# First products of a second model placed ahead of the last expert loads of the first, in a two-model kernel on one Trainium2 core

## The chip, the core and the metric

The kernel runs on one core of one Trainium2 chip. The engines that matter are TensorE (PE, with PEld for its weight loads), VectorE (DVE), ScalarE (ACT), GpSimd (POOL) and SyncE (SP, which here only issues DMA transfers, in program order, over 8 completion lanes named DMAHW0 to DMAHW7; transfers that GpSimd issues end on lanes named DMASW). A name that ends in _49 in a list of waits is a semaphore. The metric is the device time of the one core in microseconds (us), the median over several executions; lower is better.

## What is computed

Two models run one after the other, on 256 tokens of 1024 features, with 16 meta tokens ahead of them (272 columns). The first is a mixer of two attentions followed by a mixture of 32 experts (hidden size 512, two experts for each token); the second is a retention layer, a feed-forward layer, a latent attention and another feed-forward layer. Cut to what matters here:

```python
# first model
h = h + mixer(rmsnorm(h, g_mix), ...)
u = rmsnorm(h, g_ffn)                       # 256 tokens (+ 16 meta)
h = h + hier_moe(u, ...)                    # per expert: (silu(x @ w1) * (x @ w3)) @ w2
x = rmsnorm(h, g_final)[:, 16:]
# second model, first layer
h = concat(meta_2, x)
hn = rmsnorm(h, g_mix0)
proj = hn @ ret_w_in                        # q, k, v, gate of the retention
```

So between the two models stand two norms in a row, on the same sums: the mean square of the first model's output, and the mean square of that output after its gain.

## The kernel before

Activations are kept with features on the partitions, 8 blocks of 128 features by 272 columns (`h`). Weights of the mixer and of the second model are streamed as tiles of 128x128 floats, 16 tiles to a load of 1 MB (`raw`, class `Stream`) or 8 to a load of 512 KB (`rawh`); each is split into a high part on ACT (`wh`, L285) and a low part on DVE (`wl`, L286), and PE makes three products of 272 columns for each tile (L298 to L300). A tile of the activations is split likewise (`split_gain`, L289 on ACT and L290 on DVE, result `U`).

The experts (`moe`) run in 8 groups of 4 experts. A group takes 24 loads of 1 MB (`in_wm`, "chunks", 192 in all, numbered from 0): 16 for w1 and w3 (L983, 8 products each) and 8 for w2 (L1009, 8 products each). After each 4 chunks of w2 ACT copies the sum (`y`, L1012), PE scatters it to the tokens (L1016), and DVE adds it to two blocks of `h` at a time (L1018). Expert weights are not split. The chunks come through a ring of 16 slots made of three pools: `raw` (3), `raw2` (6) and `raw3` (7). `expert_fetch` (L1031) issues a chunk on SP's queue; a scheduler puts each issue where its slot becomes free.

After the second group stands a branch (L1027, L1028): when some expert has more than 32 tokens, `crowded` computes the rest. It doesn't run on these inputs, but its loads are on SP's queue, and every engine passes the branch.

In the last group (`g == 7`) `enter_meta` prepares the 16 meta columns, and `enter(b)` is called for each block as its last addition is done: it splits the block for the second model and makes two squares on ACT (L366 and L369, plain and scaled with the gain), which POOL adds up over the blocks (L373). The second model then opens with `retention`: it loads three chunks of the second stream (`in_ws2`) and two groups of constants, and `begin` (L312) computes the first four output blocks of the first projection from 8 feature blocks each: 32 tiles, 96 products, the 48 of feature blocks 0 to 3 first. Between them `enter_norms` sums the squares over the partitions (`colsum`, L383), takes the two inverse roots on DVE and spreads them over the partitions (L414). The fifth output block on PE can start when the rotations (`ro`, L1264, L1265) have freed the first accumulator.

The order on each engine is set when the kernel is built, by a scheduler that takes the program's order and the buffers' releases; the kernel's own code has no due times around the change.

## Time and profile before

| | |
|---|---|
| three runs, us | 1498.06, 1506.22, 1502.76 |
| median, us | 1502.76 |
| the profiled execution, us | 1498.93 |
| its span in the trace, us | 1497.1 |
| mixer | 0 to about 228 us |
| experts | about 229 to 692 us |
| second model | about 692 to 1497 us |
| PE busy over the span | 1314.9 us (88%) |
| bytes moved | 359.55 MB, mean 240 GB/s |

The profile is of one execution, 1498.93 us, that is 1.83 us longer than its span and 3.83 us below the median of the three. The page divides the span into 40 slices, of 37.4 us each. The mean figures over the whole span hide that the three stages have different limits, so each is to be read by itself. Places in the program are given by line, and times from the start of the span. A line "waits" gives who waited for whom, in total us, times and the longest; a bracket at the end of a row of the timeline gives the idle time of the engine before it and what ended that.

### The profile page before, as it was taken

What the parts mean: (1) busy time and instruction counts of PE and PEld (TensorE: products, weight loads), DVE (VectorE), ACT (ScalarE), POOL (GpSimd) and SP (SyncE); (2) the same over time, 40 slices, a digit from 0 to 9 for tenths busy, and PEclk for the clock granted to TensorE, in tenths of its full rate; (3) what the DMA queues carried; (4) which work ended last, traced back from release to release, by engine and by line L of the source; (5) the groups of instructions that cost most, each with busy time, mean ns of one, the idle gap of its engine ahead of it and who ended that gap; (6) DMA issues with size and microseconds to landing.
All of it is one profiled execution on the core that took longest, in us unless ns stands there. A gap on an engine that the chain in (4) does not pass through costs nothing.

```text
span 1497.1 us, 23804 instructions
## 1 busy us (share of the span) xinstructions
PE 1314.9 (88%) x9734; PEld 1051.7 (70%) x9734; DVE 724.4 (48%) x1417; ACT 528.3 (35%) x903; POOL 134.3 (9%) x165
## 2 busy tenths in 40 slices
PE   7999998776776666666999999999999999999997
PEld 7898993220221212104999999999999999899997
DVE  7866673110100101004666665766666865766654
ACT  5476651000000000004333443544444544544442
POOL 4010020000000000002121111100000211100001
PEclk9999998895787878778999999999999999999998
DMA  8443668999999999997434344454455433355551
GB/s 309 128 130 111 225 241 361 420 419 373 420 420 421 421 420 421 421 420 319 142 116 146 134 141 145 151 183 169 169 174 185 164 113 135 123 192 171 193 186 73
DMA packets 55266, 359.55 MB, mean 240 GB/s; under 512 B 6384, under 2 KB 7024, under 8 KB 15600
## 3 DMA queue, kind: packets, MB, share of 16 engines
q1 hardware_dynamic: 55152, 357.97, 63.2%
q8 instruction: 78, 1.28, 0.3%
q14 instruction: 36, 0.29, 0.1%
HBM read 356.90 MB, written 1.05 MB: 239 GB/s over the span
## 4 chain that ended last, share of the span: by engine, by line
PE 47%; DVE 2%; ACT 1%; issue 0%; POOL 0%; DVEq 0%; ACTq 0%; POOLq 0%
PE acc L298 14%; PE acc L300 14%; PE acc L299 14%; DVE wl L286 1%; ACT wh L285 1%; PE att L414 0%; PE att L1487 0%; PE att L1304 0%; PE att L1280 0%; PE att L383 0%; DVE U L290 0%; PE att L1306 0%; PE att L1397 0%; PE att L1294 0%; PE att L1305 0%
## 5 line engine op out<-in xcount | busy, mean ns | idle before, releaser
L298 PE MATMUL acc<-U,wh 128*128 128x272 f32 (+1 forms) x1456 | 424.0, 291 | 12.3 <-ACT U L289 7.2
L299 PE MATMUL acc<-U,wl 128*128 128x272 f32 (+1 forms) x1456 | 417.7, 287 | 2.5 <-DVE wl L286 2.5
L300 PE MATMUL acc<-U,wh 128*128 128x272 f32 (+1 forms) x1456 | 417.9, 287 | 0.0
L286 DVE TENSOR_TENSOR wl<-raw,wh 128x1024 fp32r<-128x1024 f32 x232 | 285.2, 1230 | 154.7 <-ACT wh L285 154.2
L285 ACT ACTIVATE wh<-raw 128x1024 fp32r<-128x1024 f32 x232 | 245.6, 1060 | 314.3 <-PE acc L300 211.2
L298 PEld LDWEIGHTS acc<-U,wh 128*128 128x128 f32 x1456 | 276.6, 190 | 17.6 <-ACT U L289 7.4
L299 PEld LDWEIGHTS acc<-U,wl 128*128 128x128 f32 x1456 | 275.9, 189 | 3.1 <-DVE wl L286 3.0
L300 PEld LDWEIGHTS acc<-U,wh 128*128 128x128 f32 x1456 | 275.9, 190 | 0.4
L983 PE MATMUL acc<-raw,U 128*32 128x512 f32 x1024 | 186.2, 820 | 91.0 <-DMA raw<-in_wm 87.3
L983 PEld LDWEIGHTS acc<-raw,U 128*32 128x32 f32 x1024 | 24.5, 124 | 238.1 <-DMA raw<-in_wm 214.7
L994 DVE TENSOR_TENSOR hid<-hid,acc 128x512 f32<-128x512 f32 x8 | 5.5, 688 | 258.1 <-PE acc L983 258.1
L300 PE MATMUL acc<-hl,wh 128*128 128x272 f32 (+1 forms) x352 | 99.5, 283 | 0.0
L299 PE MATMUL acc<-hh,wl 128*128 128x272 f32 (+1 forms) x352 | 99.3, 282 | 0.0
L298 PE MATMUL acc<-hh,wh 128*128 128x272 f32 (+1 forms) x352 | 99.1, 281 | 0.0
L1009 PE MATMUL att<-raw,ht 128*32 128x512 f32 x512 | 68.6, 635 | 28.7 <-DMA raw<-in_wm 25.1
L286 DVE TENSOR_TENSOR wl<-rawh,wh 128x512 fp32r<-128x512 f32 x112 | 80.5, 734 | 25.3 <-ACT wh L285 25.2
L285 ACT ACTIVATE wh<-rawh 128x512 fp32r<-128x512 f32 x112 | 68.2, 627 | 41.0 <-PE acc L300 24.9
L1018 DVE TENSOR_TENSOR h<-h,att 128x512 f32<-128x512 f32 x32 | 22.0, 688 | 123.9 <-PE att L1016 123.9
L298 PEld LDWEIGHTS acc<-hh,wh 128*128 128x128 f32 x352 | 66.4, 188 | 0.0
L300 PEld LDWEIGHTS acc<-hl,wh 128*128 128x128 f32 x352 | 66.1, 188 | 0.0
L299 PEld LDWEIGHTS acc<-hh,wl 128*128 128x128 f32 x352 | 66.1, 188 | 0.0
L373 POOL TENSOR_TENSOR s<-s,sq 128x256 f32<-128x256 f32 (+1 forms) x24 | 20.9, 886 | 493.3 <-ACT sq L369 492.8
(381 smaller groups left out, 1883.2 us busy)
## 6 DMA issues: line engine op xcount, KB each, us to landing
raw<-in_wm SPq DMA_DIRECT2D x192, 1024.0 KB, 19.9
raw<-in_ws SPq DMA_DIRECT2D x116, 1024.0 KB, 4.9
rawh<-in_ws SPq DMA_DIRECT2D x56, 512.0 KB, 3.9
const<-in_const SPq DMA_DIRECT2D x1, 1056.0 KB, 9.1
out<-Q SPq DMA_DIRECT2D x4, 256.0 KB, 2.5
h<-in_xt SPq DMA_DIRECT2D x2, 272.0 KB, 4.6
h<-in_xt SPq DMA_DIRECT2D x1, 544.0 KB, 6.6
small<-in_small SPq DMA_DIRECT2D x1, 512.0 KB, 6.2
```

The lines of the kernel that those rows point to most:

```text
L285: self.nc.scalar.activation(hi, src, AF.Copy)
L286: self.nc.vector.tensor_sub(lo, src, hi.bitcast(F32))
L298: mm(p[:, :n], wh, xh[:, kb, c0:c0 + n], start=kb == first, stop=False)
L299: mm(p[:, :n], wl, xh[:, kb, c0:c0 + n], start=False, stop=False)
L300: mm(p[:, :n], wh, xl[:, kb, c0:c0 + n], start=False, stop=kb == nkb - 1)
L373: self.nc.gpsimd.tensor_add(s[0], s[0], t)
L983: mm(p[32 * e:32 * e + 32], XG[:, j % 2, kb, c:c + 32], w[:, 512 * e:512 * e + 512], start=kb == 0, stop=kb == KB - 1)
L994: dve.tensor_mul(hid, hid, hh[1])
L1009: mm(p[32 * e:32 * e + 32], ht[:, f * P + e * 32:f * P + e * 32 + 32], w[:, 512 * e:512 * e + 512], start=f == 0, stop=f == 3)
L1018: dve.tensor_add(h[:, k:k + 2, NM:], h[:, k:k + 2, NM:], p.rearrange("p (j n) -> p j n", j=2))
```

## The change

- **Branch.** The loads of `crowded` are issued on GpSimd's queue instead of SP's.
- **Ring.** The pool of split weights (`wsp`, 3 pairs of tiles of 8) is made once for the whole kernel. Before, the mixer had its own with tiles of 4 and the second model its own. For this room the ring of chunks goes from 16 slots to 13 (`raw3` 7 to 4).
- **Second stream.** Its first 1 MB load is issued when 182 of the 192 expert chunks have been issued (`second_fetch`), in a slot of `raw`, and split (`Stream.split`) in the last group. Its next two loads are issued as halves of 512 KB after the last expert chunk.
- **Products.** `begin` becomes `begin_first` (the first four feature blocks of the first four output blocks, 16 tiles, 48 products), called before the last expert chunk in program order, and `begin_rest` (feature blocks 4 to 7, now block by block over the four outputs), called after the experts. The order of the tiles in memory changes with it (`_begin`).
- **Squares.** `enter` makes one square of a block instead of two, POOL adds nothing, and the sums over blocks and partitions are made by 16 small products of PE against a tile of two columns (ones and squared gain). The two spreads of the norms go into one accumulator, with two copies as before.
- **Small moves.** The meta columns' norm (`enter_meta`) is computed in group 6 instead of 7, the constants `const3` are loaded before the experts instead of after them, and in the mixer the splits are made 8 tiles at a time in two pieces.

```diff
-RAW, RAW2, RAW3 = 3, 6, 7
+RAW, RAW2, RAW3 = 3, 6, 4
...
 def _begin(blocks, cut):
-    return [b[:cut] for b in blocks[:4]] + [b[cut:] for b in blocks[:4]] + blocks[4:]
+    more = [b[k:k + 1] for k in range(cut, len(blocks[0])) for b in blocks[:4]]
+    return [b[:cut] for b in blocks[:4]] + more + blocks[4:]
...
+    def begin_first(self, ws, nkb, cut, xh, xl, cols, then=None, at=()):
         ps = [self.acc() for _ in range(3)] + [self.att()]
-        for i in range(8):
-            p, (c0, n) = ps[i % 4], cols[i % 4]
-            self.tiles(ws, p, range(cut) if i < 4 else range(cut, nkb), nkb, xh, xl, c0, n)
+        for i, (p, (c0, n)) in enumerate(zip(ps, cols)):
+            self.tiles(ws, p, range(cut), nkb, xh, xl, c0, n)
             if i in at:
                 next(then, None)
-        self.ready = [p[:, :n] for p, (_, n) in zip(ps, cols)]
+        self.begun = list(zip(ps, cols))
+
+    def begin_rest(self, ws, nkb, cut, xh, xl, then=None, at=()):
+        for kb in range(cut, nkb):
+            for p, (c0, n) in self.begun:
+                self.tiles(ws, p, [kb], nkb, xh, xl, c0, n)
+            if kb - nkb + 8 in at:
+                next(then, None)
+        self.ready = [p[:, :n] for p, (_, n) in self.begun]
...
+                if g == 6:
+                    self.consts_load("const3")
+                    self.enter_meta(m)
                 if g == 7:
-                    self.enter_meta(m)
+                    self.enter_start()
...
+                        if g == 7 and z == 1 and f == 3:
+                            self.begin_first(self.ws, KB, 4, self.u2[:, 0], self.u2[:, 1], [(0, T)] * 4)
                         w = self.expert_chunk()
...
                         if g == 7:
                             self.enter(k)
                             self.enter(k + 1)
+                            if k == 2:
+                                self.ws.split()
+                                self.ws.split()
...
+            self.ws.fetch(2, 2)
+            self.r1 = self.glob.tile([P, T], F32, name="s1")[:, :NX]
+            self.begin_rest(self.ws, KB, 4, self.u2[:, 0], self.u2[:, 1], self.enter_norms(self.r1), (4, 7))
 
     def expert_fetch(self):
 
+        if self.nraw == 192 - 192 % len(self.slots):
+
+            self.second_fetch()
...
+    def second_fetch(self):
+        self.ws = Stream(self, self.a["ws2"], 1856, self.raw, "raw", 16, 8)
+        self.ws.fetch(1)
...
-                    load = lambda c, i: nc.sync.dma_start(
+                    load = lambda c, i: nc.gpsimd.dma_start(
...
     def enter(self, b):
+
 
         x = self.h[:, b, NM:]
         self.split_gain(self.u2[:, 0, b, NM:], self.u2[:, 1, b, NM:], x, self.gg[:, b:b + 1])
-        self.square(self.s1, x, b)
-        self.square(self.s2, x, b, self.c("g_fin")[:, b:b + 1])
+        t = self.wk.tile([P, NX], F32, name="sq", bufs=4)
+        self.nc.scalar.activation(t, x, AF.Square)
+        if b == 0:
+            self.sums = self.att()
+        self.squares.append((b, t))
+        if b < 4:
+            self.sum_squares()
+
+    def sum_squares(self):
+        for b, t in self.squares:
+            for i in range(2):
+                self.nc.tensor.matmul(self.sums[:, 2 * i:2 * i + 2], t[:, i * P:(i + 1) * P], self.ones_g2[:, b],
+                                      start=b == 0 and i == 0, stop=True, skip_group_check=True)
+        self.squares = []
```

**SP at the branch.** Before, the join behind the branch waits for all eight DMA lanes, and the next expert chunk (L1036) stands behind it:

```order
L1028 UNCONDITIONAL_BRANCH [waits DMAHW0_49,DMAHW1_49,DMAHW2_49,DMAHW3_49,DMAHW4_49,DMAHW5_49,DMAHW6_49,DMAHW7_49]
L1027 ISA x2
L1036 DMA raw2_4380<-in_wm 128x2048 [waits DMAHW3_49,PE_49]
L1036 DMA raw3_4386<-in_wm 128x2048 [waits DMAHW4_49,PE_49]
L1036 DMA raw3_4392<-in_wm 128x2048 [waits DMAHW5_49,PE_49]
```

SP at the branch after the change (the branch is now L1064 and L1065, a chunk's issue L1079):

```order
L1065 UNCONDITIONAL_BRANCH
L1064 ISA x2
L1079 DMA raw2_4271<-in_wm 128x2048 [waits DMAHW4_49,PE_49]
L1079 DMA raw2_4277<-in_wm 128x2048 [waits DMAHW5_49,PE_49]
L1079 DMA raw2_4283<-in_wm 128x2048 [waits DMAHW6_49,PE_49]
L1079 DMA raw2_4289<-in_wm 128x2048 [waits DMAHW7_49,PE_49]
L1079 DMA raw2_4295<-in_wm 128x2048 [waits DMAHW0_49,PE_49]
L1079 DMA raw3_4301<-in_wm 128x2048 [waits DMAHW1_49,PE_49]
L1079 DMA raw3_4307<-in_wm 128x2048 [waits DMAHW2_49,DVE_49,PE_49]
L1079 DMA raw3_4313<-in_wm 128x2048 [waits DMASW7_49,DMASW6_49,DMAHW3_49,DMASW5_49,DMASW4_49]
```

The join has lost its waits; the seventh and eighth chunk behind it now wait for the other engines to have passed the branch.

**SP at the end of the experts.** Before, the last chunks of the experts (L1036), then the second stream's three loads (L238) and the constants (L273):

```order
L1036 DMA raw3_5574<-in_wm 128x2048 [waits DMAHW0_49,PE_49]
L1036 DMA raw3_5580<-in_wm 128x2048 [waits DMAHW1_49,PE_49]
L1036 DMA raw3_5586<-in_wm 128x2048 [waits DMAHW2_49,PE_49]
L238 DMA raw_5647<-in_ws2 128x2048 [waits DMAHW3_49,PE_49]
L238 DMA raw_5657<-in_ws2 128x2048 [waits DMAHW4_49,PE_49]
L238 DMA raw_5661<-in_ws2 128x2048 [waits DMAHW5_49,PE_49]
L273 DMA const3_5655<-in_const3 128x544 [waits DMAHW6_49,DMAHW2_49,PE_49]
L273 DMA const5_5659<-in_const5 128x2112 [waits DMAHW7_49,DMAHW1_49]
```

SP there after the change, from chunk 181 on (the second stream is L242, a chunk L1079); the "..." stands for six chunks' issues, which wait for a lane and PE:

```order
L1079 DMA raw3_5363<-in_wm 128x2048 [waits DMAHW1_49,PE_49]
L242 DMA raw_5369<-in_ws2 128x2048 [waits DMAHW2_49,PE_49]
L1079 DMA raw_5371<-in_wm 128x2048 [waits DMAHW3_49,PE_49]
L1079 DMA raw_5377<-in_wm 128x2048 [waits DMAHW4_49,PE_49]
L1079 DMA raw_5400<-in_wm 128x2048 [waits DMAHW5_49,DMAHW2_49,DVE_49]
L1079 DMA raw2_5406<-in_wm 128x2048 [waits DMAHW6_49,PE_49]
...
L1079 DMA raw3_5538<-in_wm 128x2048 [waits DMAHW4_49,PE_49]
L242 DMA raw_5570<-in_ws2 128x1024 [waits DMAHW5_49,PE_49]
```

One load of the second stream has moved ahead of ten expert chunks, and chunk 184 (`raw_5400`) takes its slot: it now waits for that load's own lane (DMAHW2) and for DVE, that is for the split of all 16 tiles.

**PE at the last chunk.** Before, the last products (L1009, chunk 191 in `raw3_5586`), the scatter of the last four blocks (L1016), and only then the second model's first products:

```order
L1009 MATMUL att_5567<-raw3_5586,ht_5500 32x512 [waits DMAHW2_49]
L1009 MATMUL att_5567<-raw3_5586,ht_5500 32x512 x3
L1016 MATMUL att_5594<-S_5502,y_5592 128x256 [waits Activation_49]
L1016 MATMUL att_5594<-S_5502,y_5592 128x256
L1016 MATMUL att_5614<-S_5502,y_5592 128x256 [waits PE_49]
L1016 MATMUL att_5614<-S_5502,y_5592 128x256
L298 MATMUL acc_5666<-U_5454,wh_5670 128x272 [waits Activation_49]
L298 MATMUL acc_5667<-U_5454,wh_5670 128x272
```

PE there after the change (second model's products L313 to L315, last chunk L1043 in `raw3_5538`, scatter L1050):

```order
L315 MATMUL att_5489<-U_5383,wh_5463 128x272
L313 MATMUL att_5489<-U_5383,wh_5463 128x272
L314 MATMUL att_5489<-U_5383,wl_5464 128x272
L315 MATMUL att_5489<-U_5383,wh_5463 128x272
L1043 MATMUL att_5467<-raw3_5538,ht_5395 32x512 [waits DMAHW4_49]
L1043 MATMUL att_5467<-raw3_5538,ht_5395 32x512 x3
L1050 MATMUL att_5546<-S_5397,y_5544 128x256 [waits Activation_49]
L1050 MATMUL att_5546<-S_5397,y_5544 128x256
L1050 MATMUL att_5558<-S_5397,y_5544 128x256 [waits PE_49]
L1050 MATMUL att_5558<-S_5397,y_5544 128x256
L313 MATMUL acc_5486<-U_5383,wh_5577 128x272 [waits Activation_49]
L314 MATMUL acc_5486<-U_5383,wl_5578 128x272 [waits DVE_49]
```

All 48 products of `begin_first` now stand ahead of chunk 191, the remaining ones behind the last scatter.

## Rows read from the trace of the kernel before

**Rows 1.** The page: mean DMA rate in each of the 40 slices; one row of the issues (KB each, median us to landing).
```profile
GB/s 309 128 130 111 225 241 361 420 419 373 420 420 421 421 420 421 421 420 319 142 116 146 134 141 145 151 183 169 169 174 185 164 113 135 123 192 171 193 186 73
...
raw<-in_ws SPq DMA_DIRECT2D x116, 1024.0 KB, 4.9
```
**Rows 2.** Windows by stage: length; busy PE, PEld, DVE, ACT, POOL; clock; DMA share; GB/s.
```profile
16.00:226.00 210.00, 208.98 (x1697) 194.36 (x1697) 150.69 (x360) 121.31 (x250) 29.86 (x34) 1.00 0.54 180
228.00:692.00 464.00, 316.80 (x1857) 88.50 (x1860) 51.73 (x151) 31.81 (x64) 1.92 (x3) 0.80 1.00 415
722.00:1497.00 775.00, 756.88 (x5986) 738.75 (x5986) 493.93 (x846) 348.80 (x541) 87.05 (x102) 0.99 0.45 153
```
**Rows 3.** Waits of SP's queue from 262 to 690 us: total us, times, longest.
```profile
SPq L1036 <- DMA raw<-in_wm: 324.3, 154, 3.5
SPq L1028 <- SPq L1028: 19.3, 3, 14.4
```
**Rows 4.** Windows around the branch, as in Rows 2.
```profile
340.00:350.00 10.00, 6.59 (x32) 0.67 (x24) 0.00 (x0) 0.00 (x0) 0.00 (x0) 0.50 0.64 238
350.00:390.00 40.00, 26.89 (x136) 5.17 (x132) 2.07 (x3) 1.88 (x3) 0.00 (x0) 0.67 1.01 420
```
**Rows 5.** Timeline of PE around the branch: chunk 52 and chunk 63.
```profile
339.61 1.94 PE L983 MATMUL acc<-raw,U 128*32 128x512 f32 x8 [1.32 <-DMA raw<-in_wm]
...
371.51 1.94 PE L983 MATMUL acc<-raw,U 128*32 128x512 f32 x8 [0.71 <-DMA raw<-in_wm]
```
**Rows 6.** Start of the experts: PE's first chunk (timeline); SP's waits, 226 to 262 us.
```profile
236.11 1.94 PE L983 MATMUL acc<-raw,U 128*32 128x512 f32 x8
...
SPq L1036 <- PE acc L983: 17.3, 10, 6.5
```
**Rows 7.** Timeline of the last groups: meta columns' norm, held-up products, last chunk.
```profile
675.60 0.15 DVE L403 TENSOR_SCALAR rs_v<-att 16x1 f32<-16x1 f32 x1 [0.37 <-PE att L383]
...
677.72 0.16 DVE L360 SCALAR_TENSOR_TENSOR rs_z<-rs_t,rs_y 128x1 f32<-128x1 f32 x1
...
680.33 5.07 PE L1009 MATMUL att<-raw,ht 128*32 128x512 f32 x32 [0.69 <-ACT ht L999]
...
691.77 1.07 PE L1009 MATMUL att<-raw,ht 128*32 128x512 f32 x8 [0.94 <-DMA raw<-in_wm]
```
**Rows 8.** Windows of 1 us, as in Rows 2: the clock behind 680 and 713 us.
```profile
683.00:684.00 1.00, 1.00 (x16) 0.26 (x12) 0.00 (x0) 0.00 (x0) 0.00 (x0) 0.87 1.02 426
...
713.00:714.00 1.00, 1.00 (x6) 1.00 (x6) 0.00 (x0) 0.16 (x1) 0.00 (x0) 0.51 1.00 426
```
**Rows 9.** Timeline from the last chunk to the fifth output block.
```profile
694.12 1.99 PE L1016 MATMUL att<-S,y 128*128 128x256 f32 x8 [1.28 <-ACT y L1012]
694.22 1.06 ACT L285 ACTIVATE wh<-raw 128x1024 fp32r<-128x1024 f32 x1 [0.15 <-DMA raw<-in_ws]
695.29 0.69 DVE L1018 TENSOR_TENSOR h<-h,att 128x512 f32<-128x512 f32 x1 [1.94 <-PE att L1016]
...
696.01 0.51 ACT L289 ACTIVATE U<-h,gg 128x256 fp32r<-128x256 f32 x1 [0.73 <-DVE h L1018]
...
696.76 1.22 DVE L286 TENSOR_TENSOR wl<-raw,wh 128x1024 fp32r<-128x1024 f32 x1
...
699.14 0.29 PE L298 MATMUL acc<-U,wh 128*128 128x272 f32 x1
...
700.14 0.29 PE L298 MATMUL acc<-U,wh 128*128 128x272 f32 x1
...
704.13 0.59 PE L298 MATMUL acc<-U,wh 128*128 128x272 f32 x1 [3.08 <-ACT wh L285]
...
704.75 0.85 PE L383 MATMUL att<-ones,s 128*128 128x1 f32 x4
...
719.53 1.05 PE L414 MATMUL att<-const,rs_z 128*128 128x128 f32 x8
...
722.59 0.36 PE L298 MATMUL acc<-U,wh 128*128 128x272 f32 x1 [2.01 <-DVE ro L1265]
```

More of the change, by code (lines that the diff above doesn't have):

```diff
@@ L237, in fetch, with split @@
             m, o = min(self.per, self.n - i) * P, i % 16 * P
-            self.k.nc.sync.dma_start(w[:, :m], self.src[i // 16][:, o:o + m])
+            e = m // pieces
+            for c in range(0, m, e):
+                self.k.nc.sync.dma_start(w[:, c:c + e], self.src[i // 16][:, o + c:o + c + e])
             self.q.append(w)
             self.c += 1
-    def next(self):
-        k, i = self.k, self.i
-        if i % self.per == 0:
+    def split(self):
+        k, j = self.k, self.j
+        if j % self.per == 0:
             if not self.q:
@@ L247, in next @@
             self.w = self.q.pop(0)
-        if i % self.cut == 0:
-            m = min(self.cut, self.n - i) * P
-            self.h = k.wsp.tile([P, self.cut * P], F32R, name="wh")
-            self.l = k.wsp.tile([P, self.cut * P], F32R, name="wl")
-            c = i % self.per * P
-            k.split(self.h[:, :m], self.l[:, :m], self.w[:, c:c + m])
+        h = k.wsp.tile([P, 8 * P], F32R, name="wh")
+        l = k.wsp.tile([P, 8 * P], F32R, name="wl")
+        n = min(8, self.n - j)
+        for o in range(0, n, self.cut):
+            m = min(self.cut, n - o) * P
+            c = (j % self.per + o) * P
+            k.split(h[:, o * P:o * P + m], l[:, o * P:o * P + m], self.w[:, c:c + m])
+        self.j += 8
+        self.parts.append((h, l))
+    def next(self):
+        i = self.i
+        if i % 8 == 0:
+            if not self.parts:
+                self.split()
+            self.h, self.l = self.parts.pop(0)
         self.i += 1
-        c = i % self.cut * P
+        c = i % 8 * P
         return self.h[:, c:c + P], self.l[:, c:c + P]
@@ L732, in mixer @@
             self.gens.append(stick())
+            qb = m.tile([P, 4, NX], F32, name="qi")
             for b in range(4):
@@ L1127, in enter_meta, with enter_start @@
         self.spread(self.row[:, :NM], self.norm_end(self.colsum([[s]], NM), NM, D, 1e-6), NM)
+    def enter_start(self):
+        self.u2 = self.glob.tile([P, 2, KB, T], F32R, name="U")
+        self.nc.vector.tensor_copy(self.h[:, :, :NM], self.meta)
+        self.split(self.u2[:, 0, :, :NM], self.u2[:, 1, :, :NM], self.meta_t)
     def enter(self, b):
```

66 lines of the change are left out of this document (34 added, 32 removed).

## The prediction, made before the changed kernel had run

> **What bounds the kernel now.** I read the windows by stage first, because the mean over the span mixes three limits. In the mixer PE is busy 208.98 of 210.00 us, in the second model 756.88 of 775.00; between them, for 464 us, it is busy 316.80 us while the DMA engines stand at a share of 1.00 and 415 GB/s [rows 2]. So the first and last stage are PE's and the experts are DMA's. The rates by slice say the same and show the hole: 420 GB/s in the experts' slices, but 373 in the tenth [rows 1]. Then I read who ends the waits of SP: in the experts it is the landing of older chunks (324.3 us), so that the next issue is never late, except at the branch, where it waits 19.3 us for its own lanes [rows 3]. Last came the timelines of the two seams, the branch and the end of the experts, since only at seams can this change take time out: a chunk of 1 MB at 421 GB/s takes 2.49 us, and nothing in the change makes one smaller. I use T for the moment at which chunk 191 lands, 691.77 in the trace [rows 7], and count to the start of the fifth output block, 722.59 [rows 9]: 30.8 us. Behind it PE is saturated as before, on the same work.
>
> **The change part by part: what moves T.**
>
> Branch: the join makes SP wait until every lane has landed, so the DMA engines run dry. From chunk 52 to chunk 63 PE's starts are 371.51 - 339.61 = 31.90 us apart [rows 5]; 11 chunks at 2.49 are 27.4, so the hole costs 4.5 us. The rate in 340 to 350 us, 238 GB/s, against 420 behind it [rows 4] says 10 x (1 - 238/420) = 4.3. The new join waits for nothing, and the first chunk that must wait for the other engines is the seventh behind it, with six transfers queued, that is 15 us of data. I take the whole 4.5 as gained (4.3 to 4.5).
>
> Second stream: its first 1 MB now goes ahead of ten chunks, in a stretch that DMA bounds: +2.49 us on T. [...]
>
> New wait: chunk 184 takes the slot of that load and waits for its landing and for both halves of its split, two of 1.06 us on ACT and 1.22 on DVE behind the second [rows 9], some 3.7 us with the handing over. Seven chunks stand behind it on SP, and PE waits for all of them. While SP waits, chunks 182 and 183 still land, the second of them 5.0 us behind the stream's load, so that the engines still have 1.3 us of work when the issue comes. A load that is issued alone lands after 4.9 us [rows 1]; 3.7 + 4.9 - 5.0 - 2.49 = 1.1 us late. The branch is the nearest row for a queue that restarts, and it lost more than its first landing; by its loss the term is 2.5. I take 2.0, nearer the branch; below it can go to 0 if the queue restarts under the rest of chunk 183, above to 4.5, the branch's whole price.
>
> Ring of 13 slots: before, SP waited at the start of the experts for PE's products 17.3 us in 10 waits [rows 6] without a gap in the transfers. With 13 slots the wait begins three chunks earlier, for the first chunk's products, which start at 236.11 us. Twelve chunks have been issued then and the last is still on its way. I take 0.2 us, range 0 to 1. Later PE consumes a chunk in 1.07 to 1.94 us [rows 5, 7] against 2.49 for a landing, and five chunks of slack beyond the eight in flight are 12.4 us, against 8.4 us from the landing of a group's last w3 chunk (T - 8 x 2.49 = 671.9) to its first w2 products at 680.33 [rows 7] in the last group, which alone has the meta norm in between.
>
> Sum for T: -4.5 + 2.5 + 2.0 + 0.2 = +0.2 us, between -2.0 and +3.5.
>
> **What moves between T and the fifth block.** Before, the path was: last products 1.07, sum copied and scatter at 694.12, addition, U of the last blocks from 696.01 on, mixed on ACT with sixteen squares and the first split; PE then starved for 3.08 us until 704.13, and ran the 96 products and 16 sums at the lower clock until 713 [rows 8, 9]. After, 48 products and half of the sums stand ahead of chunk 191, and the squares are halved. Steps, at full clock: chunk 187 lands four chunks ahead of T, at T - 10.0; 2.35 us from products to scatter, 1.2 to the addition, 0.7 addition, 0.5 for U [rows 7, 9]: first products at T - 5.3, at best T - 5.7 since the high part suffices. From there to the end of chunk 191 PE has 48 products of 0.125 (eight in 1.00 us [rows 9]), 6.0; four chunks of 1.07, 4.3; eight sums of 0.21, 1.7; the second half of a scatter, 1.0. Together 13.0: T + 7.3. So the first products don't fit before T, and the last chunk's products wait behind them. Then 1.28 to the scatter, 1.17 to the addition, 0.69 and 0.5 for addition and U [rows 9], less some 0.1 of overlap: T + 10.8. The other 48 products 6.0, eight sums 1.7, 0.6 of waiting for U of later blocks: T + 19.1. The norms' chain is 14 small operations of VectorE at 0.2 us (12 in 2.3 us [rows 7]), released by the last sums and mostly beside the last products; 0.8 remains. Spread 1.05, then 2.0 to the rotations' release [rows 9]: T + 23.0. Against 30.8 this gives 7.8 us.
>
> The weights of the later products come by two loads in halves behind the last chunk; the first half is wanted at T + 10.8 and has been landed for several us, so cost nothing. Removed additions on POOL and eight squares on ACT count only in that they no longer sit between U and the splits; they are in the steps above. The mixer's splits by eight, the earlier constants (544 floats on each partition, under a mixer that moves 180 GB/s [rows 2]) and the meta norm in group 6 lie beside PE or DMA work: 0, at most 1 us either way in the mixer, where PE is the bound and its products are the same.
>
> **The clock** decides between these steps and slower ones. The w2 products that began at 680.33 ran at the lower clock until 683.25 (0.87 in that slice: from 0.50 to 1.00), after 3 us without a pause; behind 704.13 the lower clock lasted until 714, over 9 us [rows 7 to 9]. Before the first products, PE will do one chunk of 1.07 to 1.94 us in each 2.49. I take 4 us of the lower clock from the first products on, near the 3 us case, since the products come without a pause: what takes 0.125 took about 0.227 there, so 1.8 us are lost. T + 24.8, a gain of 6.0 us.
>
> Total: +0.2 - 6.0 = **-5.8 us**. The profiled execution would go from 1498.93 to 1493.1; it is 3.8 us under the median of the runs, which would go from 1502.76 to **1497.0**.
>
> **Rivals.**
>
> Full clock and a short restart: the first products find the higher clock and chunk 184 costs the 1.1 us; T by -0.9, the tail by -7.8: -8.7 us, 1494.1. For it speaks that from 684 on the clock was full through the last chunk; against it that the held-up w2 products that brought it there are spread out now, as the meta norm leaves group 7.
>
> Half clock for longer: as behind 704.13, 9.4 us at the lower clock cost 4.2 instead of 1.8: -3.4 us, 1499.4. [...]
>
> The products in the way, on the other side: if the lower clock holds through all of it, the 48 products ahead of chunk 191 take 10.9, the four chunks 7.8, sums and scatter 3.6; the last chunk ends at T + 16.6, the last U at T + 20.9, the other products and sums 13.2 later, the fifth block at T + 39, 8 us later than now: +8.4 us, 1511.2. It turns to a loss once the lower clock lasts over some 17 us; against it, PE is then busy without a pause, and both rows end the lower clock within 10 us of that.
>
> The hole at the branch stays: SP stops there for another reason (the branch itself, or chunks 62 and 63 that wait for the others), and 4.5 isn't gained: -1.3, 1501.5. Against it: of the 19.3 us SP's wait is for its own lanes.
>
> **How the numbers follow.** Forecast 0.45; full clock 0.27; longer half clock 0.12; hole stays 0.08; products in the way 0.05; 0.03 for a loss from the ring or the restart above my bounds. The median of three runs here can be off by some 4 us, as the three lie over 8. Half a per cent, 7.5 us, is about what a measurement of this kernel can tell from no change: faster needs 1495.2. The forecast falls below that 3 times in 10, the full-clock case 2 in 3: 0.35 with a little of the rest. Slower 0.07, the rest 0.58. Range: 1489.0 (full clock, 5 us of scatter) to 1504.0 (hole stays, or longer half clock, with scatter).
>
> **What would show it.** In the changed kernel: no dip of the rate near 345 us and chunks at 2.49 us there; a hole of about 2 us in the transfers behind chunk 183; T within 3 us of 691.8; PE's products of the second model ahead of T, their spacing (0.125 or 0.227) telling the clock; the last chunk's products about 7 us behind its landing, and the fifth block 23 to 27 us behind it. Wrong would be: a rate under 400 GB/s elsewhere in the experts, last chunk's products over 15 us late, or a second model longer than 775 us.

## The result, and the profile after

The changed kernel took 1493.09 us (median of 5 runs, 1488.68 to 1497.56) against 1502.76 of the kernel before, run beside it (5 runs, 1498.06 to 1506.22): a ratio of 0.9941, 95% interval 0.9918 to 0.9964, a gain of 9.7 us. A second comparison on another chip (under a_after below) gave 0.9965 [0.9947, 0.9984], 5.9 us. The forecast was 5.8 us. The sum and the measurement thus lie close together, but the steps show that part of this is two errors of opposite sign.

The profiled execution took 1488.68 us, the fastest of the five. The page of the kernel after: its span and the DMA rate in each of 40 slices, to be put beside [rows 1]:

```profile
span 1487.0 us, 23794 instructions
...
GB/s 309 133 127 112 217 261 300 425 426 425 426 426 426 426 427 426 427 396 359 117 138 143 127 133 155 153 172 171 173 176 184 165 114 124 132 188 183 197 193 63
```

Three things differ from [rows 1]. The dip in the tenth slice is gone (373 before, 425 now). The seventh slice is lower (300 against 361) and the eighteenth has a new dip (396). And every full slice in between stands at 425 to 427, where before it stood at 419 to 421. Nothing in the change was meant to do the last.

Windows of the kernel after (columns as in [rows 2]): the experts and the second model as wholes, then the start of the experts, the branch, a long undisturbed stretch, and the end of the experts:

```profile
228.00:692.00 464.00, 327.12 (x1893) 95.05 (x1892) 54.57 (x160) 34.20 (x65) 0.00 (x0) 0.79 1.00 417
722.00:1487.00 765.00, 747.04 (x5938) 729.74 (x5937) 485.60 (x831) 347.78 (x540) 82.91 (x98) 0.99 0.45 154
...
230.00:240.00 10.00, 5.16 (x27) 2.83 (x31) 6.77 (x43) 0.80 (x3) 0.00 (x0) 0.66 0.81 315
240.00:250.00 10.00, 10.00 (x78) 3.94 (x71) 1.00 (x3) 1.15 (x3) 0.00 (x0) 1.00 0.96 360
...
340.00:350.00 10.00, 5.58 (x28) 0.64 (x24) 0.00 (x0) 0.00 (x0) 0.00 (x0) 0.66 1.01 424
380.00:640.00 260.00, 182.85 (x1024) 50.82 (x1020) 24.87 (x61) 14.18 (x26) 0.00 (x0) 0.79 1.01 426
660.00:670.00 10.00, 5.72 (x24) 0.60 (x24) 2.36 (x2) 2.00 (x2) 0.00 (x0) 0.50 0.81 318
...
665.00:666.00 1.00, 0.29 (x4) 0.20 (x8) 1.00 (x2) 0.20 (x1) 0.00 (x0) 0.50 0.66 279
```

340 to 350 us runs at 424 GB/s, where [rows 4] had 238. The two prices stand beside it: 315 and 360 GB/s in the first 20 us of the experts, and 318 behind chunk 183. The second begins ahead of the next issue: from 665 to 666 us, with only chunks 182 and 183 left to land, the rate is down to 279, and chunk 184 is issued at 666.68.

SP's waits in the kernel after (total us, times, longest), the first row from 226 to 262 us, the others from 262 to 700; they answer to [rows 3, 6]:

```profile
SPq L1079 <- PE acc L1012: 19.7, 12, 8.6
...
SPq L1079 <- DMA raw<-in_wm: 315.9, 153, 2.6
SPq L1079 <- DMA raw<-in_ws: 14.2, 1, 14.2
SPq L1079 <- PEq L1065: 6.8, 1, 6.8
SPq L1079 <- DVE wl L301: 3.5, 1, 3.5
```

At the branch SP still waits once, 6.8 us for PE's sequencer, but with six transfers queued that shows in no rate. At chunk 184 it waits for the second stream's load (14.2) and then 3.5 us for DVE's half of the split; the second is what empties the engines.

The timeline of the kernel after, at the start and the end of the experts (chunk 0; the splits, chunk 184's issue, chunk 187; first products; then, behind the last landing, the half-load's split, the last chunk and the fifth block):

```profile
237.11 1.91 PE L1012 MATMUL acc<-raw,U 128*32 128x512 f32 x8
...
663.20 2.00 ACT L300 ACTIVATE wh<-raw 128x1024 fp32r<-128x1024 f32 x2 [14.38 <-DMA raw<-in_ws]
664.29 2.36 DVE L301 TENSOR_TENSOR wl<-raw,wh 128x1024 fp32r<-128x1024 f32 x2 [31.89 <-ACT wh L300]
666.68 4.03 SPq L1079 DMA_DIRECT2D raw<-in_wm  x8
678.90 1.07 PE L1043 MATMUL att<-raw,ht 128*32 128x512 f32 x8 [1.42 <-DMA raw<-in_wm]
683.19 0.39 PE L313 MATMUL acc<-U,wh 128*128 128x272 f32 x1 [1.32 <-ACT U L304]
691.56 1.06 ACT L300 ACTIVATE wh<-raw 128x1024 fp32r<-128x1024 f32 x1 [4.13 <-DMA raw<-in_ws]
696.58 1.07 PE L1043 MATMUL att<-raw,ht 128*32 128x512 f32 x8
713.84 0.60 PE L313 MATMUL acc<-U,wh 128*128 128x272 f32 x1 [2.25 <-DVE ro L1328]
```

PE is busy with the early products when chunk 191 lands, so its landing has no row of its own. At 691.56 ACT starts on the half-load that stands right behind chunk 191; half a megabyte at 426 GB/s is 1.23 us, so T = 690.3. Against the 691.77 of [rows 7] T has moved by -1.5 us. The fifth block starts at 713.84, T + 23.5, against 722.59 and T + 30.8 [rows 9]. The whole gain up to the fifth block is 8.75 us: 1.5 on T, 7.3 behind it. The rest of the span, 773.2 us against 774.5, does the same work as before.

### The profile page after: what moved, and what is told of

Same layout as the page of the kernel before. It is cut to its first block, busy times and chain, and to the rows that moved or that the text cites. A ratio compares the mean times of both kernels' runs of the same rounds, so it can differ in the third digit from the quotient of the medians.

```text
span 1487.0 us, 23794 instructions
## 1 busy us (share of the span) xinstructions
PE 1317.5 (89%) x9750; PEld 1048.3 (71%) x9750; DVE 722.1 (49%) x1419; ACT 522.0 (35%) x895; POOL 124.4 (8%) x153
## 4 chain that ended last, share of the span: by engine, by line
PE 49%; DMA 22%; DVE 3%; ACT 1%; issue 1%; POOL 0%; SPq 0%; DVEq 0%; ACTq 0%; POOLq 0%
DMA raw<-in_wm 22%; PE acc L313 14%; PE acc L315 14%; PE acc L314 14%; DVE wl L301 1%; ACT wh L300 1%; PE att L440 1%; PE att L1550 0%; PE att L1367 0%; PE att L1343 0%; DVE U L305 0%; PE att L409 0%; PE att L1043 0%; PE att L1369 0%; PE att L1460 0%
## 5 line engine op out<-in xcount | busy, mean ns | idle before, releaser
L313 PE MATMUL acc<-U,wh 128*128 128x272 f32 (+1 forms) x1456 | 423.2, 291 | 11.6 <-ACT U L304 9.2
L315 PE MATMUL acc<-U,wh 128*128 128x272 f32 (+1 forms) x1456 | 416.6, 287 | 0.4 <-DVE U L305 0.4
L313 PEld LDWEIGHTS acc<-U,wh 128*128 128x128 f32 x1456 | 275.7, 189 | 17.6 <-ACT U L304 10.2
L315 PEld LDWEIGHTS acc<-U,wh 128*128 128x128 f32 x1456 | 275.4, 189 | 2.8 <-DVE h L1052 0.8
L315 PE MATMUL acc<-hl,wh 128*128 128x272 f32 (+1 forms) x352 | 99.4, 283 | 0.0
L313 PE MATMUL acc<-hh,wh 128*128 128x272 f32 (+1 forms) x352 | 99.1, 281 | 0.0
L1043 PE MATMUL att<-raw,ht 128*32 128x512 f32 x512 | 74.5, 680 | 23.6 <-DMA raw<-in_wm 19.4
L300 ACT ACTIVATE wh<-rawh 128x512 fp32r<-128x512 f32 x112 | 65.0, 624 | 33.8 <-PE acc L315 20.4
L313 PEld LDWEIGHTS acc<-hh,wh 128*128 128x128 f32 x352 | 66.3, 188 | 0.0
L315 PEld LDWEIGHTS acc<-hl,wh 128*128 128x128 f32 x352 | 66.2, 188 | 0.0
L313 PE MATMUL acc<-yh,wh 128*128 128x272 f32 (+1 forms) x192 | 56.7, 295 | 3.2 <-DVE h L362 3.2
```

The costliest lines, as they stand in the source:

```text
L300: self.nc.scalar.activation(hi, src, AF.Copy)
L313: mm(p[:, :n], wh, xh[:, kb, c0:c0 + n], start=kb == first, stop=False)
L315: mm(p[:, :n], wh, xl[:, kb, c0:c0 + n], start=False, stop=kb == nkb - 1)
L1043: mm(p[32 * e:32 * e + 32], ht[:, f * P + e * 32:f * P + e * 32 + 32], w[:, 512 * e:512 * e + 512], start=f == 0, stop=f == 3)
```

## The experiments

The theories. **By the steps:** the gain is the branch (about -4.4) and the end of the experts (-6 to -7), paid for with the moved load, its wait and a little of the ring. **Rivals:** the rate of 426 GB/s, which is worth 6.2 us over 445 us, comes from the ring, from the branch's queue or from elsewhere, and is the larger part of the gain; and the early products, which cost a load ahead of ten chunks, carry no gain at all.

**The kernel before again (e0_before),** unchanged, as the bound on what a comparison can show.

> The kernel before, unchanged, to have its transfer rate beside the others on one chip. After the change the experts' transfers ran at 426 GB/s against 420 in the trace of before, which over 445 us is some 6 us. If that is the chip or the day, this run shows 426 too, with the hole at the branch still there; if it comes from the change, it shows 420 again. Time: ratio 1.000 within 0.003.

Measured: 1501.82 us (10 runs), ratio 1.0003 [0.9990, 1.0016]. Its windows, for the comparisons on this chip:

```profile
230.00:240.00 10.00, 4.83 (x24) 2.70 (x24) 6.82 (x42) 0.80 (x3) 0.00 (x0) 0.66 0.93 365
240.00:250.00 10.00, 10.00 (x77) 3.88 (x76) 1.27 (x3) 1.15 (x3) 0.00 (x0) 1.00 1.02 428
...
380.00:640.00 260.00, 185.19 (x1013) 53.58 (x1008) 22.78 (x48) 14.17 (x26) 0.00 (x0) 0.77 1.01 421
```

**The short ring alone (e1_ring):** the kernel before with 13 slots.

```diff
-RAW, RAW2, RAW3 = 3, 6, 7
+RAW, RAW2, RAW3 = 3, 6, 4
```

> The kernel before with a ring of 13 slots instead of 16, nothing else. My theory: a ring of 13 runs dry at the start of the experts, because the last of its first 13 chunks has landed before the first chunk's products free a slot; a gap of 2 to 3.5 us near 238 us, the rest as before: +2 to +3.5 us. Rival: the ring is also what makes the transfers faster (426 instead of 420 GB/s): then -6 us with it, so -2.5 to -4.

Measured: 1504.80 us, ratio 1.0025 [1.0008, 1.0043], 3 us slower. Windows of this kernel:

```profile
230.00:240.00 10.00, 4.64 (x29) 2.81 (x27) 7.52 (x45) 1.70 (x5) 0.00 (x0) 0.68 0.72 301
240.00:250.00 10.00, 10.00 (x76) 4.33 (x76) 1.27 (x3) 1.15 (x3) 0.00 (x0) 0.98 0.83 299
...
380.00:640.00 260.00, 186.12 (x1007) 54.18 (x1007) 21.42 (x46) 14.78 (x27) 0.00 (x0) 0.76 1.01 420
```

In the first 20 us the rate is 301 and 299 where e0_before has 365 and 428: (64 + 129) x 10 / 420 = 4.6 us of transfers lost. The ring is not free, and it is not what raised the rate: that stays at 420.

**The branch's queue alone (e2_branch, e2_again):** the kernel before with the rare path's loads on GpSimd's queue, timed in two sets.

```diff
-                    load = lambda c, i: nc.sync.dma_start(
+                    load = lambda c, i: nc.gpsimd.dma_start(
```

> The kernel before with the loads of the rare path on GpSimd's queue, nothing else. My theory: the hole of the transfers at the branch goes, and with it 4.5 us: -4.5 us (-4.0 to -5.0), no dip of the rate near 345 us. Rival one: the branch is also what sets the rate behind it, then 426 GB/s and -8 to -10 us. Rival two: SP stops there anyway, 0.

> The kernel before with the rare path's loads on GpSimd's queue, for a second set of times and a second trace: in the first set the trace had no hole and its fifth block 5.6 us earlier, but the median was only 1.2 us lower (ratio 0.998 to 1.002). If the hole is worth its 4.4 us, the ratio is 0.997 here; if it is worth 1 us, 0.9993, and something gives it back: then PE's own wait at the branch is longer, or chunks land behind it with a new gap, in this trace or the earlier.

Measured: 1500.62 us, ratio 1.0000 [0.9984, 1.0017] in the first set; 1496.35 us, 0.9958 [0.9939, 0.9976] in the second, on another chip. Windows of e2_branch, and its chunks 52 and 63 in the timeline of PE, to be put beside [rows 4, 5]:

```profile
340.00:350.00 10.00, 5.80 (x24) 0.63 (x24) 0.00 (x0) 0.00 (x0) 0.00 (x0) 0.50 1.02 421
380.00:640.00 260.00, 176.72 (x1008) 48.97 (x1008) 22.77 (x48) 13.59 (x25) 0.00 (x0) 0.81 1.01 421
```
```profile
340.43 1.93 PE L983 MATMUL acc<-raw,U 128*32 128x512 f32 x8 [1.43 <-DMA raw<-in_wm]
...
368.13 1.93 PE L983 MATMUL acc<-raw,U 128*32 128x512 f32 x8 [0.55 <-DMA raw<-in_wm]
```

The hole is gone in the traces of both (421 and 419 GB/s in 340 to 350), and the rate of the experts is that of before. From chunk 52 to chunk 63 PE's starts are 27.70 us apart, against 31.90 in [rows 5]: 4.2 us less. The two intervals do not overlap, so the sets differ by more than their own scatter explains; together they say some 3 us, between 0 and 6. That the hole closes is shown; that its 4.4 us arrive whole at the end is compatible with the times and no more.

**The branch's queue undone (e3_sync):** the kernel after with these loads back on SP's queue (the line above, the other way round).

> The changed kernel with the loads of the rare path back on SP's queue. My theory: the hole at the branch comes back and costs 4.5 us: the time is some 5 us below before instead of 9.7, ratio 0.997. If the branch's queue sets the rate, it falls back to 420 GB/s as well, and the time is at or above that of before.

Measured: 1499.37 us, ratio 0.9977 [0.9959, 0.9995]. Windows of this kernel:

```profile
350.00:360.00 10.00, 4.92 (x32) 0.61 (x24) 0.00 (x0) 0.00 (x0) 0.00 (x0) 0.71 0.66 250
380.00:640.00 260.00, 175.56 (x1016) 46.43 (x1016) 24.17 (x60) 14.18 (x26) 0.00 (x0) 0.82 1.01 426
```

The hole is back (250 GB/s), and the rate is still 426: the queue of the rare path doesn't set it either. The gain over the kernel before, 2.5 us, is 3.4 to 7.2 us below the two that were measured for the kernel after (5.9 and 9.7), in other sets.

**The kernel after again (a_after),** on another chip, in one set with the next three.

> The changed kernel, unchanged, on the chip of the next three, which are to be compared with it: ratio 0.994 to before (0.992 to 0.996). Chunks in the pools raw and raw3 land 2.43 us apart, those in raw2 2.48, the fifth block starts 23 to 24 us behind the last chunk's landing.

Measured: 1496.48 us (12 runs, 1491.41 to 1502.87), ratio 0.9965 [0.9947, 0.9984]; 3.4 us more than in the first set. Its timeline of the half-load behind the last chunk and of the fifth block:

```profile
691.03 1.06 ACT L300 ACTIVATE wh<-raw 128x1024 fp32r<-128x1024 f32 x1 [4.06 <-DMA raw<-in_ws]
...
714.57 0.39 PE L313 MATMUL acc<-U,wh 128*128 128x272 f32 x1 [2.25 <-DVE ro L1328]
```

T is about 689.8, and the fifth block starts at T + 24.8. The granted clock stood at 0.50 from 705 to 708 us.

**The moved load in another slot (e4_shift):** the kernel after, with the slots' order shifted by one from the moved load on, so that the chunk that must wait for the split comes a whole round later.

```diff
-        name = self.slots[self.nraw % len(self.slots)]
+        name = self.slots[(self.nraw + (self.nraw >= 182)) % len(self.slots)]
```

> The changed kernel, with the last ten chunks moved one slot on in the ring, so that chunk 184 no longer takes the slot of the second stream's load and waits for its split. My theory: the hole of 2.6 us in the transfers behind chunk 183 goes, the last chunk lands 2.6 us earlier, and everything behind it follows: -2.6 us against the changed kernel, ratio 0.992. Rival: PE, already 6 us behind at the last chunk, gets the chunks earlier but the products no earlier: 0 to -1.

Measured: 1492.67 us (6 runs, 1490.03 to 1497.64), ratio 0.9937 [0.9912, 0.9961], 3.8 us under a_after, though the two intervals overlap. The trace is of its slowest run. Its windows, and its timeline of the first products, the last chunk and the fifth block:

```profile
660.00:670.00 10.00, 4.89 (x24) 0.56 (x24) 2.89 (x3) 2.31 (x3) 0.00 (x0) 0.66 1.02 430
...
690.00:692.00 2.00, 2.00 (x6) 0.86 (x4) 0.00 (x0) 0.00 (x0) 0.00 (x0) 0.50 1.04 436
```
```profile
682.50 0.59 PE L313 MATMUL acc<-U,wh 128*128 128x272 f32 x1 [1.32 <-ACT U L304]
...
703.85 1.06 PE L1043 MATMUL att<-raw,ht 128*32 128x512 f32 x8
...
721.09 0.60 PE L313 MATMUL acc<-U,wh 128*128 128x272 f32 x1 [2.25 <-DVE ro L1328]
```

The hole is gone (430 against 318 GB/s), and T comes at about 687.2, 2.6 us ahead of a_after's. But in this execution the granted clock stood at 0.50 from 679.7 to 699.7 us, the last 17 of them, from the first products on, with PE at work without a pause. The last chunk's products then began at T + 16.6 and the fifth block at T + 33.9: the rival "products in the way" in its first half (it had the end of the last chunk at T + 16.6 and the fifth block at T + 39), in one execution, whose 1497.64 us were still below the kernel before.

**Without the early products (e6_end):** the kernel after, with the second stream's first load, its splits and all of `begin` behind the experts, in the order in which the kernel before has them; everything else stays.

```diff
-                        if g == 7 and z == 1 and f == 3:
-                            self.begin_first(self.ws, KB, 4, self.u2[:, 0], self.u2[:, 1], [(0, T)] * 4)
...
-                            if k == 2:
-                                self.ws.split()
-                                self.ws.split()
...
+            self.second_fetch()
+            self.begin_first(self.ws, KB, 4, self.u2[:, 0], self.u2[:, 1], [(0, T)] * 4)
             self.ws.fetch(2, 2)
...
-        if self.nraw == 192 - 192 % len(self.slots):
...
-            self.second_fetch()
```

> The changed kernel without early products: the second stream's first load, its splits and the first 48 products stand behind the last chunk again; one square per block, the ring, the branch stay. My theory: the last chunk lands 5.1 us earlier (no load of 2.46 ahead of it, no hole of 2.6), but PE then idles until the first split and the last addition, and starts the 96 products some 5.5 us behind the landing: 12 us of them, sums, norms and spread at full clock give a fifth block 22.5 to 23.5 us behind the landing, that is 4 to 5 us earlier than the changed kernel; at the lower clock, as in the kernel before, 27 to 29, that is 0 to +1. Rival, the change's own idea: the early products carry the gain of 7 us behind the last chunk, and without them the fifth block comes 28 to 31 us behind the landing: 0 to +3 against the changed kernel.

Measured: 1488.88 us (6 runs, 1486.98 to 1491.73), ratio 0.9917 [0.9895, 0.9939]: 7.6 us faster than a_after in the same set, with intervals that do not overlap. Its timeline of chunk 187, the last chunks and the fifth block:

```profile
675.99 1.07 PE L1041 MATMUL att<-raw,ht 128*32 128x512 f32 x8 [1.42 <-DMA raw<-in_wm]
...
689.60 1.92 PE L1041 MATMUL att<-raw,ht 128*32 128x512 f32 x16
...
712.82 0.36 PE L313 MATMUL acc<-U,wh 128*128 128x272 f32 x1 [2.34 <-DVE ro L1322]
```

Chunk 187 lands at 675.99, and four more chunks at 2.46 us give T, about 685.8, 4.0 us ahead of a_after's. The load (2.5) and the hole that it brought (some 2.5 by e4_shift) are worth more than that, but this execution lost part of it at the start of the experts, with 329 GB/s from 240 to 250 us against 356 in a_after. The fifth block starts at T + 27.0 instead of T + 24.8. So in these two traces the early products take 2.2 us out of the stretch behind T, and cost 4.0 ahead of it. That is a net of 1.75 us in the fifth block's start. Another 4.0 us lie behind it, where both kernels do the same work (772.5 us to the end of the span in this trace, 776.5 in a_after's): 1.0 directly behind the fifth block, where a_after's clock stands at 0.50 from 715 to 718 us, 1.0 near 1290 us, where its mean clock from 1265 to 1325 us is 0.97, with 1.00 at both places in e6_end, and 2 behind 1410 us, with the clock at 1.00 in both. Whether the kernel has a part in these falls is not shown. The rest of the medians' 7.6 us is in neither trace.

**Shift and split products (e7_both):** e4_shift, with 36 of the early products ahead of chunk 191 and the other 12 between the two pairs of the last scatter.

```diff
...
-                            self.begin_first(self.ws, KB, 4, self.u2[:, 0], self.u2[:, 1], [(0, T)] * 4)
+                            parts = self.begin_parts(self.ws, KB, 4, self.u2[:, 0], self.u2[:, 1], [(0, T)] * 4)
+                            next(parts)
+                            next(parts)
...
+                    if g == 7 and z == 1:
+                        next(parts)
...
+                            if k == 4:
+                                list(parts)
```

> As e4_shift, and of the 48 first products only 36 stand ahead of the last chunk, the other 12 between the two pairs of the last scatter, where PE waited for additions. My theory: the last chunk's products end 1.5 us earlier and the gap behind the scatter is filled: -1.5 us against e4_shift, -4 against the changed kernel, ratio 0.991. Rival: the second pair of the scatter comes 1.5 us later, and with it the last two blocks and their sums: 0 against e4_shift.

Measured: 1490.82 us (9 runs), ratio 0.9936 [0.9911, 0.9960], not to be told from e4_shift. In its trace the clock stood at 0.50 from 683 to 690 us only; the last chunk's products began at 696.93 and the fifth block at 714.89. That the place of the products matters less than what an execution's clock does around them fits this, and isn't shown.

**The chunks' addresses (e8_align):** the kernel before with three unused tiles ahead of the pools of chunks, which change where a chunk begins on each partition. The tiles allocated behind a pad move with it, and three memsets come in; nothing else changes. In bytes modulo 512: `raw` 448 to 128, `raw2` 480 to 0, `raw3` 448 to 256. In the kernel after, whose new pools moved them, they are 0, 352 and 0.

```diff
+            self.pad = g.tile([P, 48], F32, name="pad")
+            nc.vector.memset(self.pad, 0.0)
             self.h = g.tile([P, KB, T], F32, name="h")
...
+            pad2 = self.moectx.enter_context(tc.tile_pool(name="pad2", bufs=1, side="right")).tile([P, 120], F32, name="pad2")
+            dve.memset(pad2, 0.0)
...
+            pad3 = pool("pad3").tile([P, 32], F32, name="pad3")
+            dve.memset(pad3, 0.0)
```

> The kernel before, with only the addresses of its chunk pools moved by small unused tiles: raw from 448 to 128 bytes past a multiple of 512 on each partition, raw2 from 480 to 0, raw3 from 448 to 256. In the changed kernel raw and raw3 lie at multiples of 512, raw2 at 352, and the chunks of the first two land some 2.43 us apart, of raw2 2.48. My theory: the address of the destination sets the rate. Then raw2's chunks land 2.43 us apart here; raw's and raw3's too if 128 or 256 is enough, 2.49 if not: 6 of 16 chunks at 0.055 us is -4 us in all, 16 of 16 some -10 us (ratio 0.9935). Rival: the rate is set by something else in the change (the queue of the rare path is ruled out, the ring too): 2.49 everywhere and 0.

Measured: 1494.14 us, ratio 0.9939 [0.9922, 0.9956], 8 us faster by the pads alone. Windows of this kernel:

```profile
340.00:350.00 10.00, 5.74 (x32) 0.62 (x24) 0.00 (x0) 0.00 (x0) 0.00 (x0) 0.67 0.63 240
380.00:640.00 260.00, 182.63 (x1028) 50.77 (x1024) 22.82 (x48) 14.18 (x26) 0.00 (x0) 0.79 1.01 427
```

The branch's hole is there as before (240 GB/s), and the rate is 427. With the spacing of the chunks by pool, in the last section, that settles where the rate of the kernel after comes from.

**All of it together (e10_best):** the kernel after with 16 slots again (the split weights' pool made once for the mixer and once for the second model), the early load and products taken out as in e6_end, and a pad of 352 bytes so that all three pools of chunks begin at 0 modulo 512.

```diff
-RAW, RAW2, RAW3 = 3, 6, 4
+RAW, RAW2, RAW3 = 3, 6, 7
...
-            self.wsp = pool("wsp", 3)
...
+            self.wsp = pool("wsp1", 3)
...
+            self.moectx.enter_context(tc.tile_pool(name="pad2", bufs=1, side="right")).tile([P, 88], F32, name="pad2")
...
+            self.wsp = pool("wsp2", 3)
```

> A version put together from the findings: the changed kernel's branch, squares, sums and early constants, but the split weights in pools of the mixer and of the second model again, so that the ring has 16 slots; the second stream's first load and the first products behind the last chunk; and all three pools of chunks at multiples of 512 bytes. Against the variant without early products (1488.9): no gap at the start of the experts, -3.5; raw2's chunks at 2.43 instead of 2.48, -4. The last chunk lands at 675 to 678 us, the time is 1479 to 1483, ratio 0.986. Rival: PE can't follow at 431 GB/s with the lower clock, and half of it is lost: 1486.

Measured: 1487.93 us (6 runs, 1485.59 to 1490.36), ratio 0.9899 [0.9881, 0.9917], where 1479 to 1483 were expected: 14.3 us faster than the kernel before, and faster than the kernel after, whose interval (a_after, the same chip in another set) lies wholly above. Its windows, and chunk 187 and the fifth block in its timeline:

```profile
230.00:240.00 10.00, 5.38 (x27) 3.16 (x31) 6.28 (x41) 0.80 (x3) 0.00 (x0) 0.51 1.00 399
380.00:640.00 260.00, 184.48 (x1030) 50.68 (x1029) 24.17 (x60) 13.58 (x25) 0.00 (x0) 0.77 1.01 427
```
```profile
670.77 1.94 PE L1042 MATMUL att<-raw,ht 128*32 128x512 f32 x8 [1.44 <-DMA raw<-in_wm]
...
712.65 0.36 PE L313 MATMUL acc<-U,wh 128*128 128x272 f32 x1 [2.34 <-DVE ro L1324]
```

No hole is left, T comes at about 680.6 (chunk 187 lands at 670.77, four more follow at 2.45), and yet the fifth block starts at 712.65, T + 32, no sooner than in e6_end. In this trace the sums of squares stood on PE between the pairs of a scatter, ahead of chunks that had landed, and the clock was 0.50 from 671 to 684 and again from 694 to 701.

**The sums later (e12_sums):** e10_best with the sums of the first four blocks behind the last chunk's first scatter, so that the last chunk has PE when it lands.

```diff
-        if b < 4:
-            self.sum_squares()
...
+        if b == 4:
+            self.sum_squares()
```

> The version put together before, with one thing moved: the sums of the first four blocks' squares stand on PE behind the last chunk's first scatter instead of between the two scatters of chunk 187, where PE, in order, waited for ACT's squares and held chunk 188 for some 4.5 us. My theory: that wait was why the earlier landing (679 us by my reading) gave nothing at the fifth block (712.65, 34 us behind): now the last chunk's products follow its landing within 2 us and the fifth block comes 23 to 29 us behind it, at 702 to 708: -5 to -10 us against the version before it (1487.9), ratio 0.984 to 0.987. Rival: the lower clock alone made PE late, and the order doesn't matter: 0 to -2.

Measured: 1486.93 us (6 runs, 1486.08 to 1492.03), ratio 0.9913 [0.9893, 0.9933], no gain over e10_best that can be told. The trace is of its slowest run. Its timeline of the last chunk and the fifth block, and a window:

```profile
683.57 1.06 PE L1042 MATMUL att<-raw,ht 128*32 128x512 f32 x8 [1.36 <-DMA raw<-in_wm]
...
714.77 0.36 PE L313 MATMUL acc<-U,wh 128*128 128x272 f32 x1 [2.34 <-DVE ro L1324]
```
```profile
690.00:692.00 2.00, 2.00 (x8) 1.73 (x8) 0.00 (x0) 0.00 (x0) 0.00 (x0) 0.50 0.68 284
```

The last chunk's products now begin when it lands, as wanted. But the clock stood at 0.50 from 686 to 703 us, with PE busy but for 0.8 us, and the fifth block came at T + 31, not at the 23 to 29 that were expected.

## Why the prediction was right, and where it was not

**The branch: right.** -4.5 was taken; at 424 GB/s in 340 to 350 us it is 10 x (1 - 238/424) = 4.4, and e2 and e3 switch it on and off. PE waits 5.2 us at the new branch and SP 6.8, with six transfers queued, as reckoned.

**The moved load: right.** 1 MB at 426 GB/s is 2.5 us, as taken.

**The wait at chunk 184: right within 0.5 us.** 2.0 was taken; 318 GB/s in 660 to 670 us says 10 x (1 - 318/426) = 2.5. The split took the 3.5 us that were reckoned as 3.7, and the hole cost more than the simple account of 1.1, which has the engines full until chunk 183 lands, while the rate was 279 from 665 to 666 us. e4_shift removes it, and T comes 2.6 us earlier.

**The ring: the step that failed.** 0.2 us was taken, at most 1; it cost 3.2. The step assumed that the twelfth chunk would still be on its way when PE's first products freed a slot. But ten of the thirteen chunks that the ring holds had landed under the mixer: from 230 to 240 us, at 315 GB/s, just 3.15 MB moved, that is three chunks. The engines were dry from 238.2 until a freed slot's chunk was issued at 239.09 and landed later, 3.2 us of transfers in all. The mixer's last part and chunk 0's products also came 1.0 us later (237.11 against 236.11 [rows 6]), which needn't be the ring's: in e0_before, the kernel before, chunk 0's products came at 237.44. What looked like slack, SP's waits of 17.3 us without a gap [rows 6], was three slots deep, and the change took exactly three. e1_ring shows the same by itself: 4.6 us of transfers, 3 us of time.

**The rate: not foreseen.** From 420 to 426 GB/s over the 445 us from 245 to 690 is 445 x (1 - 420/426) = 6.2 us (5.2 with the 421 that the windows from 380 to 640 us have). The prediction held "nothing in the change makes one smaller" to be enough; pools that moved by some bytes made the chunks faster. e8_align shows this alone, with 427 GB/s from 380 to 640 us against the 421 of e0_before.

**T: close by two errors.** -4.4 (branch) + 2.5 (load) + 2.5 (wait) + 3.2 (ring) + 1.0 (later start of the experts) - 6.2 (rate) = -1.4, good to about 1 us, where the trace has -1.5 and the forecast had +0.2. Without the rate T would have been 4.7 us late, outside the bounds of -2.0 to +3.5.

**Behind T: close, again with errors inside.** The last chunk's products began at T + 6.3 and ended at T + 7.35 (T + 7.3 taken). But the first products of the second model came at T - 7.1 (683.19) instead of T - 5.3 to T - 5.7, since chunk 187 landed 11.4 us ahead of T and not 10.0, and from there to the end of the last chunk PE took 14.5 us instead of 13.0; the two cancel. The fifth block came at T + 23.5 (T + 24.8 taken with 4 us of the lower clock, T + 23.0 at the full one). The granted clock was 1.00 from 676 to 713 us, so this execution is the full-clock rival's in its tail, and 0.5 us of the steps was short. In a_after, with the lower clock from 705 to 708 us, it was T + 24.8.

**The clock's bound: wrong.** The chance of 0.05 for "products in the way" rested on two rows in which the lower clock ended within 10 us of unbroken work [rows 7 to 9]. e4_shift had 17 us of it without a pause, e12_sums 17 with one pause of 0.8 us, and e4_shift's last chunk fell back to T + 16.6. Both traces are of the slowest of 6 runs, and neither kernel's median shows the loss, so the case seems to belong to an execution more than to a kernel; other executions of these two were not traced.

**What the early products were worth.** The prediction put the whole tail into one term. e6_end splits it: without the early products the fifth block stands at T + 27.0, so 3.8 us of the gain (from T + 30.8) come without them, and the early products bring 2.2 more (to a_after's T + 24.8), less than the 4.0 us that they cost ahead of T. These are single executions, whose clocks differ: behind 704 us the kernel before had over 9 us at 0.50 [rows 8, 9], worth 4.2 by the prediction's own reckoning, and e6_end had 1.00 there, from 688 us on. So whether the 3.8 come from the cheaper squares, from the sums on PE, from the small moves or from the clock is not shown; no run changed one of them alone. Of the parts that a run switched by itself, the chunks' addresses (6.2) and the branch (4.4) gained the most.

Left open: why the clock falls in one execution and not in another, where the 2 us between a_after and e6_end behind 1410 us come from, and why the two sets of e2 differ by 4 us. Runs of one kernel differ by 5 to 12 us from the lowest to the highest; between traces, falls of the clock behind the experts and the end of the mixer differ by some us. What sets those was not found.

## What to carry to other kernels

Before a ring of buffers is cut, count how many of its slots are loaded ahead of the consumer's first step, not how long the issuer waits without a gap: the slots that are landed when the consumer starts are the reserve. Here ten of thirteen had landed, and the engines were dry from 238.2 us until the first freed slot's chunk was issued at 239.09. In a stretch bound by large transfers, look up the addresses at which the destination tiles begin before moving work around: pads of 128 to 480 bytes were worth 8 us in e8_align, where the whole rearrangement gained 9.7 and 5.9. And work moved ahead of the last transfers had two prices here, its own load in the bound stretch (2.5 us) and the wait of the chunk that took its buffer (2.5 us); put both beside what the tail can give.

## What the hardware showed that I had not expected

**The address of the destination changed a transfer's time by 2%.** Between landings of consecutive chunks of 1 MB (8 KB on each of 128 partitions), medians by pool: before, 2.48 to 2.49 us in all three (448, 480 and 448 bytes modulo 512); after, 2.44 and 2.43 in `raw` and `raw3` (0 and 0) and 2.48 in `raw2` (352); e8_align 2.49 in `raw` (128), 2.43 and 2.44 in `raw2` and `raw3` (0 and 256); e10_best 2.44 to 2.45 in all three (0). So the pools that began at 0 or 256 bytes modulo 512 went at 2.43 to 2.45, those at 128, 352, 448 and 480 at 2.48 to 2.49. It can be read in a row of PE's waits in the kernel after, chunks 124 and 125 in `raw2`, 126 to 128 in `raw3`:

```profile
519.95 1.06 PE L1012 MATMUL acc<-raw,U 128*32 128x512 f32 x8 [1.42 <-DMA raw<-in_wm]
522.44 1.94 PE L1012 MATMUL acc<-raw,U 128*32 128x512 f32 x8 [1.42 <-DMA raw<-in_wm]
524.85 1.94 PE L1012 MATMUL acc<-raw,U 128*32 128x512 f32 x8 [0.48 <-DMA raw<-in_wm]
527.28 1.89 PE L1012 MATMUL acc<-raw,U 128*32 128x512 f32 x8 [0.49 <-DMA raw<-in_wm]
529.71 1.07 PE L1012 MATMUL acc<-raw,U 128*32 128x512 f32 x8 [0.54 <-DMA raw<-in_wm]
```

Within `raw2` the starts are 2.49 apart, within `raw3` 2.43. The 2% is measured for the address that is written, since the pads of e8_align move where a chunk lands and not where it is read. No run tells how it comes about.

**The lower clock lasted through 17 us of unbroken work.** Before the clock rose, PE had worked without a pause at 0.50 for 3 us and for over 9 us in the kernel before [rows 7 to 9], and for 17 in e4_shift. How long the next stretch would last could not be read from the last.

**The queue that ran out lost more than its wait and the next landing.** The hole behind chunk 183 took 2.5 us of transfers, where the waiting and one landing alone account for 1.1. Part of it lay ahead of the next issue at 666.68: from 665 to 666 us, with two chunks left to land, the rate was 279 GB/s.
